# RG-LRU constants made beside S5's first parameters, the first layer norm by ScalarE's square root, and Newton's step on one column with one tensor operand

## The chip, the core and the metric

The kernel runs on one core of a Trainium2 chip. Its engines are TensorE (PE, with the weight loads shown as PEld), VectorE (DVE), ScalarE (ACT), GpSimd (POOL) and SyncE (SP, which here issues all DMAs). Each engine works through its own list of instructions in a fixed order; engines wait for each other by semaphores. The metric is the device time of one execution in microseconds (us), lower is better.

## The reference, cut to what matters

One layer of a trunk: a projection feeds three mixers side by side, their outputs are normalized in groups and projected back, a layer norm follows, then a gated convolutional MLP and a second layer norm. Input and output are 1024 tokens of 1024 values in float32.

```python
proj = x @ w_in[l] + b_in[l]
q, k, v, u, xr, gate = jnp.split(proj, SPLITS, axis=-1)
y_attn = sliding_window_attention(rope(q), rope(k), v, attn_sinks[l])
y_s5  = s5_mixer(u, ...)          # complex diagonal state space model, 16 groups of 64 states
y_lru = rg_lru_mixer(xr, gate, ...)
mix = group_rmsnorm((y_attn, y_s5, y_lru), mix_norm_g[l])
x = layer_norm(ALPHA * x + mix @ w_out[l] + b_out[l], ln1_g[l], ln1_b[l])
f = conv_gated_mlp(x, ...)
x = layer_norm(ALPHA * x + f, ln2_g[l], ln2_b[l])

# in rg_lru_mixer: a constant of each channel, from a_param alone
log_a = -LRU_C * ga * jax.nn.softplus(-a_param)
# in layer_norm
y = xc * lax.rsqrt(var + LN_EPS) * g + b
```

## The kernel before

Matrices are multiplied in three passes over split operands: every float32 operand is a high part `hi`, rounded by ACT, and a low part `lo`, the difference, made mostly by DVE (`split`, L115 to L123: ACT at L119, DVE at L120), and `mm3` (L140) issues hi x hi, lo x hi and hi x lo (L144 to L146). A projection weight is loaded as `wraw`, then split into `whi` and `wlo` (`wsplit`, L166).

The kernel starts with the projection of `u`, the input of S5 (L1292 to L1309), then runs the other projections one half of 512 tokens at a time (`project`, L1319; order in `ORDER`). The work of the mixers is cut into steps of generators, and `AGENDA` says after which projection or attention unit each step is taken (`side`, L1384). `self.after(...)` ties the instructions written inside it to an earlier instruction for the planner only: no semaphore comes of it.

The order on each engine is made by a planner when the kernel is built. It takes ready instructions, those written earlier first, by its own picture of the times, and it hands out tile buffers too. Small tiles (up to 64 bytes in a partition) come from one pool of 64 buffers, by `self.small`.

S5's parameters are made in `s5` (L242), a generator. Its first part (L242 to L263) makes `s5dt`, `s5ang`, `s5n`, `s5r` and `s5x` from the packed parameters, its second (L264 to L274) sines, `decay` and a reciprocal, its third (L275 to L306) the powers `s5Pr`, `s5Pi` and the input matrix `s5Br`, `s5Bi`. The fourth and fifth (L308 to L317) make `s5CA` and `s5W`, 1024 columns each: three operations of each product on DVE (L228 to L230), three on POOL (L231 to L233), and `s5CAi` is negated on DVE at L313. PE then multiplies them at L331 (`s5kp`) and transposes at L341 (`s5wt`).

`lru_setup` (L530) makes the constants of the RG-LRU from two columns: an exponential (`acc_exp`, L200, tiles `lre`), a reciprocal and a polynomial, 33 small DVE instructions and one DMA. They are needed by the gates of `lru` (L582). The call stands at L1313, behind S5's third part (L1312) and the second weight split (L1311).

For a norm, `ln_stats` (L838) makes the mean and variance and a first guess of the reciprocal root, either by POOL's power (`pow`, L797) or by ACT's square root and DVE's reciprocal (L845, L846); `newton` (L800) then improves it by one step. The first layer norm (L1408 to L1417) takes the power, the second (L1496, L1514) the root. In the first, each block of 128 rows goes through `out_group`, statistics, guess, Newton and a normalization (L1416); PE then transposes the block in `x1_block` (L858), and its transposed form feeds the MLP. In the second norm `norm` (L1452) makes `lnm`, lets ACT scale the block, and DVE and POOL take one half of it each (L1462, L1463); the last block is finished by DVE alone (L1515 to L1524).

Of the kernel before, what the change touches and what calls it, by code (L numbers as in the profile page):

```python
# [15 lines left out]
MULT, ADD, SUB, MAX, MIN = ALU.mult, ALU.add, ALU.subtract, ALU.max, ALU.min  # L16
# [41 lines left out]
ALPHA = 2.0 ** 0.25  # L58
LN_EPS = 1e-5
# [18 lines left out]
class Trunk:  # L78
# [721 lines left out]
    def newton(self, r, a):  # L800
        v = self.nc.vector
        t = self.small(list(a.shape), "rst")
        if a.shape[1] == 1:
            v.scalar_tensor_tensor(t, r, a, r, MULT, MULT)
        else:
            v.tensor_tensor(out=t, in0=r, in1=a, op=MULT)
            v.tensor_tensor(out=t, in0=t, in1=r, op=MULT)
        v.tensor_scalar(t, t, -0.5, 1.5, MULT, ADD)  # L808
        v.tensor_tensor(out=r, in0=r, in1=t, op=MULT)

# [417 lines left out]
    def mixers(self):  # L1228
# [7 lines left out]
        r = self.r  # L1236
# [14 lines left out]
        def load_w(h, a, b):  # L1251
            if a == 0:
                ws[h] = self.big([128, NK, 128], "uraw")
            return nc.sync.dma_start(out=ws[h][:, a:b], in_=I["w_in"][6 + h][:, a:b])
# [8 lines left out]
        first = load_w(0, 0, 2)  # L1263
# [15 lines left out]
        def u_out(h, hf, p):  # L1279
            nc.scalar.activation(ud[h][:, :, hf * 64:hf * 64 + 64], p.rearrange("p (c j) -> p j c", j=T5),  # L1280
                                 AF.Identity, bias=self.col("b_in", 6 + h))

        def u_half(h, hf):
            u_out(h, hf, self.proj_half(W[h], self.X, hf, "pud"))
        gs5 = self.s5(ud)
        for f, *a in ((split_w, 0, 0, 2), (split_x, 0, 0), (split_w, 1, 0, 2), (split_w, 0, 2, NK), (split_x, 0, 1),
# [3 lines left out]
            first = self.hi  # L1290
# [11 lines left out]
        self.wsplit(1)  # L1302
        with self.after(first.ins):
            next(gs5)
        u_half(0, 1)
        self.s5_bounce(0, ud[0])
        next(gs5)
# [2 lines left out]
        W = None  # L1310
        self.wsplit(2)  # L1311
        next(gs5)  # L1312
        with self.after(first.ins):  # L1313
            self.lru_setup()
        xr, self.gg, self.q = [], [], []
        steps = [(n[:-1], int(n[-1]), ORDER[:j].count(n)) for j, n in enumerate(ORDER)]
        at, done, Ws = {}, {}, {}
# [66 lines left out]
        def side(t):  # L1384
            with self.after(self.mm.ins):
                for n, g in gens.items():
                    for _ in range(AGENDA[n].count(t)):
                        next(g, None)
# [19 lines left out]
        for tb in range(NB):  # L1408
            self.out_group((0, 1, 2, 3), Wa, MA, r[0], tb)
            z = self.z[tb]  # L1410
            bn = self.small([128, 2, 6], "st")
            for h in range(2):
                nc.vector.bn_stats(bn[:, h], z[:, h * 512:(h + 1) * 512])
            mv, a, rs = self.ln_stats(bn, LN_EPS / ALPHA ** 2)
            self.newton(rs, a)
            nc.vector.tensor_scalar(z, z, mv[:, 0:1], rs, SUB, MULT)  # L1416
            side(100 + tb)  # L1417

    def ffn(self, out):
        nc = self.nc  # L1420
        v = nc.vector
# [24 lines left out]
        st, bn = {}, {}  # L1446
# [5 lines left out]
        def norm(tb):  # L1452
            z = self.z[tb]
            mv, a, r = st[tb]
            self.newton(r, a)
            m = self.small([128, 1], "lnm")
            v.scalar_tensor_tensor(m, mv[:, 0:1], -1.0, r, MULT, MULT)
            o = self.big([128, D], "o")
            for h, e in enumerate((v, nc.gpsimd)):
                s = hs[h]  # L1460
                nc.scalar.activation(z[:, s], z[:, s], AF.Identity, scale=r, bias=m)
                e.tensor_tensor(out=z[:, s], in0=z[:, s], in1=g2[:, s], op=MULT)  # L1462
                e.tensor_tensor(out=o[:, s], in0=z[:, s], in1=b2[:, s], op=ADD)  # L1463
                if tb == 2:
                    nc.sync.dma_start(out=out[0, tb * 128:(tb + 1) * 128, s], in_=o[:, s])
            if tb != 2:
                nc.sync.dma_start(out=out[0, tb * 128:(tb + 1) * 128, :], in_=o)

        cut = nd - self.LAST
        for i in range(cut):  # L1470
# [28 lines left out]
            if p == 3 and 0 < f < 5:  # L1499
                with self.after(self.mm.ins):  # L1500
                    norm(3 + f)
        T = ps["T"]
        self.d_parts(nd)
        for c in range(4):
            last = c == 3
            for k, s in enumerate((slice(0, 256), slice(256, 512)) if last else (hs[0],)):
                for i in range(cut, nd):
                    self.d_product(i, T, (c,), False, i == nd - 1, s)
                    if i == cut and c and not k:
                        with self.after(self.mm.ins):  # L1510
                            norm(c - 1)
                self.d_out(3, c, T, s)
                stats(c, 1 + k, slice(512 + s.start, 512 + s.stop))
            st[c] = self.ln_stats(bn[c][:, 0:2 + last], LN_EPS, True)  # L1514
        tb = 3  # L1515
        z = self.z[tb]
        mv, a, r = st[tb]
# [82 lines left out]
```

## Time and profile before

| | |
|---|---|
| median of 3 runs | 1032.95 us (1032.45 to 1208.34) |
| the profiled execution | 1030.83 us, span of its instructions 1028.9 us |
| PE busy | 969.5 us |
| DVE busy | 770.3 us |
| POOL busy | 557.1 us |
| ACT busy | 488.0 us |

The span runs from the first to the last instruction; the execution's own time has a little around it. Busy time counts what an engine executes, waits for a busy memory interface included, so a DVE instruction can look long because it stood still. A timeline row gives the start and the length in us, the engine, the line of the kernel, the operation, the tile written and the tiles read, shapes, the number of instructions merged in the row, and in brackets the idle time in front of it and what ended it.

### The profile page before, as it was taken

The page shows a single profiled execution, that of the slowest core. Times are in us where ns is not written, and L with a number is a line of the kernel's source. Part 1 is how long each engine was busy: PE and PEld are TensorE (multiplying, and loading weights), DVE is VectorE, ACT ScalarE, POOL GpSimd, SP SyncE. Part 2 cuts the span into 40 slices and gives each one's busy share as a digit, 9 for nine tenths or more (in the row PEclk, how much of TensorE's full clock was granted, in tenths as well). Part 3 has the DMA queues.
Part 4 walks back from the last instruction along what each step waited for, and adds up shares of the span by engine and source line. Part 5 has one row for each costly group of instructions (what it writes and reads, how often), then busy time and mean ns, then how long its engine had stood idle before and what let it go on. Part 6 is the DMA issues. An engine that isn't in the chain of part 4 may idle for free.

```text
span 1028.9 us, 13343 instructions
## 1 busy us (share of the span) xinstructions
PE 969.5 (94%) x4512; PEld 794.4 (77%) x4512; DVE 770.3 (75%) x1254; ACT 488.0 (47%) x943; POOL 557.1 (54%) x417
## 2 busy tenths in 40 slices
PE   9699889989999898899999999999999999999993
PEld 6588757879888676678878778888887788888873
DVE  6969767699888777677677677665676699965298
ACT  6121258667762675535435445445447265444131
POOL 0504405559944684767886978653561799000053
PEclk9899889999999999999999999999999999999997
DMA  8413483443231201447546546412415798686113
GB/s 298 143 42 85 112 205 97 113 129 113 83 124 46 99 20 42 154 161 268 206 162 245 226 154 244 156 59 95 147 78 184 284 391 276 213 293 189 62 42 122
DMA packets 64740, 158.53 MB, mean 154 GB/s; under 512 B 9440, under 2 KB 14080, under 8 KB 64672
## 3 DMA queue, kind: packets, MB, share of 16 engines
q1 hardware_dynamic: 64672, 157.68, 44.8%
q8 instruction: 35, 0.57, 0.2%
q14 instruction: 33, 0.27, 0.1%
HBM read 104.90 MB, written 42.21 MB: 143 GB/s over the span
## 4 chain that ended last, share of the span: by engine, by line
PE 49%; DVE 16%; POOL 13%; DMA 9%; issue 8%; ACT 5%; SPq 1%; DVEq 0%; POOLq 0%; ACTq 0%
PE pg L144 7%; PE pg L146 6%; PE pg L145 6%; PE pdT L145 3%; DMA d<-in_ffn_w_down_dram 3%; PE pdT L146 3%; PE pdT L144 3%; PE pdQ L144 2%; PE pdQ L146 2%; POOL dt L1126 2%; PE pdQ L145 2%; POOL d L1126 2%; PE pin L146 1%; PE pin L144 1%; PE pin L145 1%
## 5 line engine op out<-in xcount | busy, mean ns | idle before, releaser
L120 DVE TENSOR_TENSOR dpl<-draw,dph 128x1024 fp32r<-128x1024 f32 x77 | 120.1, 1598 | 30.1 <-ACT dph L119 28.3
L144 PE MATMUL pg<-xt,apart 128*128 128x512 f32 x352 | 137.3, 391 | 3.6 <-ACT foa L1004 1.4
L145 PE MATMUL pg<-xt,apart 128*128 128x512 f32 x352 | 137.3, 390 | 1.4 <-DVE xt L930 1.4
L146 PE MATMUL pg<-xt,apart 128*128 128x512 f32 x352 | 136.3, 391 | 2.0 <-DVE apart L120 1.9
L119 ACT ACTIVATE dph<-draw 128x1024 fp32r<-128x1024 f32 x77 | 80.1, 1058 | 86.6 <-DVE dpl L120 28.1
L120 DVE TENSOR_TENSOR apart<-s,apart 128x512 fp32r<-128x512 f32 x88 | 93.0, 1067 | 25.3 <-ACT apart L119 25.3
L144 PE MATMUL pg<-xb,apart 128*128 128x512 f32 x264 | 103.2, 391 | 1.4 <-ACT fob L1004 1.4
L145 PE MATMUL pg<-xb,apart 128*128 128x512 f32 x264 | 102.8, 389 | 0.0
L146 PE MATMUL pg<-xb,apart 128*128 128x512 f32 x264 | 102.7, 389 | 0.0
L119 ACT ACTIVATE apart<-s 128x512 fp32r<-128x512 f32 x88 | 53.8, 625 | 84.5 <-POOL s L939 62.4
L144 PEld LDWEIGHTS pg<-xt,apart 128*128 128x128 f32 x352 | 66.1, 188 | 19.7 <-ACT foa L1004 3.6
L146 PEld LDWEIGHTS pg<-xt,apart 128*128 128x128 f32 x352 | 66.1, 188 | 18.3 <-DVE apart L120 4.9
L1462 POOL TENSOR_TENSOR z<-z,ln_g 128x512 f32<-128x512 f32 x7 | 10.9, 1556 | 124.9 <-DVE rst L808 111.4
L145 PEld LDWEIGHTS pg<-xt,apart 128*128 128x128 f32 x352 | 66.1, 188 | 15.8 <-DVE xt L930 2.3
L120 DVE TENSOR_TENSOR apart<-raw,apart 128x512 fp32r<-128x512 f32 x66 | 71.4, 1082 | 5.7 <-ACT apart L119 5.7
L145 PE MATMUL pdT<-dpl,dph 128*128 128x512 f32 (+1 forms) x182 | 69.9, 384 | 2.2 <-DVE dpl L120 2.2
L146 PE MATMUL pdT<-dph,dpl 128*128 128x512 f32 (+1 forms) x182 | 69.4, 382 | 0.0
L144 PE MATMUL pdT<-dph 128*128 128x512 f32 (+1 forms) x182 | 66.7, 383 | 0.7 <-DVE z L1203 0.5
L144 PEld LDWEIGHTS pg<-xb,apart 128*128 128x128 f32 x264 | 49.6, 188 | 12.6 <-ACT fob L1004 2.2
L146 PEld LDWEIGHTS pg<-xb,apart 128*128 128x128 f32 x264 | 49.6, 188 | 10.3
L145 PEld LDWEIGHTS pg<-xb,apart 128*128 128x128 f32 x264 | 49.6, 188 | 10.2
L1060 POOL TENSOR_TENSOR fc<-fc,fob 128x512 f32<-128x512 f32 x11 | 18.7, 1702 | 71.2 <-DVE fob L1003 62.8
(482 smaller groups left out, 2627.0 us busy)
## 6 DMA issues: line engine op xcount, KB each, us to landing
draw<-h SPq DMA_DIRECT2D x77, 256.0 KB, 5.4
raw<-in_ffn_w_gate_dram SPq DMA_DIRECT2D x22, 512.0 KB, 5.0
raw<-in_ffn_w_up_dram SPq DMA_DIRECT2D x22, 512.0 KB, 4.2
h<-fc SPq DMA_DIRECT2D x22, 512.0 KB, 2.6
d<-in_ffn_w_down_dram SPq DMA_DIRECT2D x22, 512.0 KB, 6.6
draw<-d SPq DMA_DIRECT2D x44, 256.0 KB, 5.4
draw<-in_ffn_w_down_dram SPq DMA_DIRECT2D x33, 256.0 KB, 5.4
h<-hs SPq DMA_DIRECT2D x11, 512.0 KB, 3.6
```

Of the source, the lines that this page charges most:

```text
L119: self.hi = nc.scalar.activation(hi, src, AF.Copy)
L120: e.tensor_tensor(out=lo, in0=src, in1=hi.bitcast(F32), op=SUB)
L144: self.mm = nc.tensor.matmul(out, ah, bh, start=first, stop=False, skip_group_check=more)
L145: nc.tensor.matmul(out, ah, bl, start=False, stop=False, skip_group_check=more)
L146: nc.tensor.matmul(out, al, bh, start=False, stop=last, skip_group_check=more)
L1060: e.tensor_tensor(out=c[:, one], in0=c[:, one], in1=x, op=MULT)
L1126: sub = lambda o, a, b: po.tensor_tensor(out=o, in0=a, in1=b, op=SUB)
L1462: e.tensor_tensor(out=z[:, s], in0=z[:, s], in1=g2[:, s], op=MULT)
```

## The change

Four edits. `lru_setup` is called right behind S5's first part, under the same `after`, and no longer behind its third part. The first layer norm passes `True` to `ln_stats`: ACT's square root and DVE's reciprocal take the place of POOL's power. In `newton`, where the operand has one column, the three instructions become `tensor_scalar` with one tensor operand and the others as per-partition scalars; operands of four columns keep theirs. In the second norm `lnm` is made in the same way.

```diff
@@ newton @@
         if a.shape[1] == 1:
-            v.scalar_tensor_tensor(t, r, a, r, MULT, MULT)
-        else:
-            v.tensor_tensor(out=t, in0=r, in1=a, op=MULT)
-            v.tensor_tensor(out=t, in0=t, in1=r, op=MULT)
+            v.tensor_scalar(t, r, a, r, MULT, MULT)
+            v.tensor_scalar(t, t, -0.5, 1.5, MULT, ADD)
+            v.tensor_scalar(r, r, t, None, MULT)
+            return
+        v.tensor_tensor(out=t, in0=r, in1=a, op=MULT)
+        v.tensor_tensor(out=t, in0=t, in1=r, op=MULT)
         v.tensor_scalar(t, t, -0.5, 1.5, MULT, ADD)
         v.tensor_tensor(out=r, in0=r, in1=t, op=MULT)
@@ mixers @@
         self.wsplit(1)
         with self.after(first.ins):
             next(gs5)
+            self.lru_setup()
         u_half(0, 1)
@@
         self.wsplit(2)
         next(gs5)
-        with self.after(first.ins):
-            self.lru_setup()
@@ first layer norm @@
-            mv, a, rs = self.ln_stats(bn, LN_EPS / ALPHA ** 2)
+            mv, a, rs = self.ln_stats(bn, LN_EPS / ALPHA ** 2, True)
             self.newton(rs, a)
@@ norm, second layer norm @@
-            v.scalar_tensor_tensor(m, mv[:, 0:1], -1.0, r, MULT, MULT)
+            v.tensor_scalar(m, mv[:, 0:1], r, -1.0, MULT, MULT)
```

## Rows read from the trace of the kernel before

**Rows 1.** The page, busy us, share of the span, instructions of engines.

```profile
PE 969.5 (94%) x4512; PEld 794.4 (77%) x4512; DVE 770.3 (75%) x1254; ACT 488.0 (47%) x943; POOL 557.1 (54%) x417
```

**Rows 2.** Waits of PE, whole span: us in total, times, longest us.

```profile
PE pin L146 <- DVE wlo L120: 7.9, 1, 7.9
PE xp L109 <- DVE z L1416: 6.2, 3, 3.8
...
PE pdT L145 <- DVE dpl L120: 2.2, 2, 1.7
```

**Rows 3.** Windows: length, busy PE, PEld, DVE, ACT, POOL, PEclk, DMA share, GB/s.

```profile
354.00:359.00 5.00, 4.14 (x16) 3.52 (x17) 2.42 (x8) 2.81 (x8) 0.63 (x2) 0.66 0.44 183
45.00:55.00 10.00, 4.93 (x12) 3.87 (x13) 9.41 (x26) 0.00 (x0) 5.61 (x8) 0.50 0.16 64
```

**Rows 4.** Timeline of PE in the projections, columns as told above.

```profile
50.07 0.79 PE L146 MATMUL pin<-xah,wlo 128*128 128x512 f32 x1 [7.88 <-DVE wlo L120]
...
71.59 0.41 PE L331 MATMUL s5kp<-s5CAi,s5B 128*32 128x128 f32 x2
```

**Rows 5.** Timeline of DVE in the same stretch.

```profile
26.17 0.16 DVE L262 TENSOR_TENSOR s5x<-s5dt,s5lr 128x8 f32<-128x8 f32 x1
...
26.72 0.17 DVE L206 TENSOR_SCALAR s5e_x<-s5x 128x8 f32<-128x8 f32 x1
...
27.95 1.18 DVE L213 SCALAR_TENSOR_TENSOR s5e_p<-s5e_p,s5e_r 128x8 f32<-128x8 f32 x6
...
32.76 0.16 DVE L539 TENSOR_SCALAR lrn<-pack 128x2 f32<-128x2 f32 x1
...
38.27 0.28 DVE L233 TENSOR_TENSOR s5Bi<-s5Bi,s5bbt 128x128 f32<-128x128 f32 x1
...
40.69 7.13 DVE L213 SCALAR_TENSOR_TENSOR lre_p<-lre_p,lre_r 128x2 f32<-128x2 f32 x6
...
48.80 1.21 DVE L120 TENSOR_TENSOR wlo<-wraw,whi 128x1024 fp32r<-128x1024 f32 x1
49.94 0.15 DVE L546 TENSOR_SCALAR lrp<-lrq 128x2 f32<-128x2 f32 x1
50.00 0.15 DVE L550 TENSOR_SCALAR lrs<-lrn 128x2 f32<-128x2 f32 x1
...
65.36 0.69 DVE L313 TENSOR_SCALAR s5CAi<-s5CAi 128x1024 f32<-128x1024 f32 x1
```

**Rows 6.** Timeline of POOL in the same stretch.

```profile
33.16 1.94 POOL L231 TENSOR_TENSOR s5CAi<-s5Pr,s5pack 128x1024 f32<-128x1024 f32 x1 [18.85 <-DMA s5U<-du]
...
45.25 2.33 POOL L233 TENSOR_TENSOR s5Wi<-s5Wi,s5wt 128x1024 f32<-128x1024 f32 x1
```

**Rows 7.** Timelines of DVE and POOL in the first layer norm.

```profile
341.48 0.15 DVE L808 TENSOR_SCALAR rst<-rst 128x1 f32<-128x1 f32 x1
341.67 1.03 DVE L809 TENSOR_TENSOR rs<-rs,rst 128x1 f32<-128x1 f32 x1
...
341.39 1.29 POOL L938 TENSOR_TENSOR s<-raw 128x512 f32<-128x512 f32 x1
```

**Rows 8.** Timeline of DVE at the first norm's sixth block.

```profile
347.51 0.15 DVE L843 TENSOR_SCALAR lna<-mv 128x1 f32<-128x1 f32 x1
...
351.37 0.67 DVE L804 SCALAR_TENSOR_TENSOR rst<-rs,lna 128x1 f32<-128x1 f32 x1 [2.21 <-POOL rs L798]
```

**Rows 9.** ACT: its timeline before the blocks; line L845, ns min/median/max.

```profile
327.07 1.16 ACT L119 ACTIVATE apart<-s 128x512 fp32r<-128x512 f32 x2 [20.59 <-POOL s L941]
...
L845 ACT ACTIVATE rs<-lna x8: 185/202/203, 983.1 to 1020.5; 128x1 f32<-128x1 f32 x8
L845 ACT ACT_TABLE_LOAD  x1: 1283/1283/1283, 956.8 to 956.8; - x1
```

**Rows 10.** Line L804, ns min/median/max; timeline of DVE in the tail.

```profile
L804 DVE SCALAR_TENSOR_TENSOR rst<-rs,lna x16: 203/680/1327, 316.5 to 1022.8; 128x1 f32<-128x1 f32 x16
...
1022.85 1.21 DVE L804 SCALAR_TENSOR_TENSOR rst<-rs,lna 128x1 f32<-128x1 f32 x1
```

## The prediction

> **What bounds the kernel now.** I read the page's busy table first: TensorE (PE) works 94% of the span [rows 1]. So a saving anywhere else is worth only what it takes out of PE's remaining idle time, or off the last microseconds, in which PE has nothing left. Next I read PE's waits [rows 2], longest first, to see which idle time the change can reach. Three entries matter. One wait of 7.9 us is for `wlo`, the low part of a projection weight made by VectorE (DVE). Three waits, 6.2 together and 3.8 the longest, are for `z`, the row block normalized by the first layer norm. Two waits, 2.2 together, are for `dpl` near the end. Then the windows [rows 3]: behind the first wait the granted clock is 0.50 for ten microseconds with 4.93 us of matmuls, behind the 3.8 us wait it is 0.66 over five. PE's two levels are 1.2 and 2.4 GHz; in both stretches it fell after PE had stood still and came back once PE worked again. Work at the lower level takes twice as long, so the first stretch lost 4.93 / 2 = 2.5 us and the second (3.4 of 5 us at half speed) 1.7. What can be won is thus 7.9 + 2.5 = 10.4 at the first place, 6.2 + 1.7 = 7.9 at the second, and something in the tail. All of it would be 1.8% of the time and a little.
>
> **Why wlo is late.** In DVE's timeline [rows 5] the first instruction of `lru_setup` (`lrn`) starts at 32.76, and `wlo` follows only at 48.80, behind most of it. Six instructions of the exponential take 1.18 us for S5 at 27.95 (0.20 each, one waiting for the other), and the same six take 7.13 us for the RG-LRU at 40.69. What differs is POOL: its products and differences over 1024 columns run nearly back to back from 33.16 on [rows 6] (first and last of six). One POOL instruction that runs from 341.39 for 1.29 us shows the rule [rows 7]: a one-column instruction with one tensor operand takes 0.15 us beside it, the next one, with two, takes 1.03 and ends when POOL's ends. So a two-tensor instruction waits for POOL's to end.
>
> **Part 1, lru_setup moved.** Its DMA stays early (weights `lw`, one issue, needed only by the gates much later). Its 33 DVE instructions move ahead of S5's second part, into a stretch in which POOL stands still: no waits there. But they don't come free. In [rows 5] `s5e_x` of S5's second part needs only `s5x` (26.17), yet starts at 26.72; and `lrs` needs only `lrn` (32.76), yet starts at 50.00, right behind `lrp` (49.94). The planner hands out small tiles in the order of the program's first writes. Moved, `lrs` stands ahead of all of S5's second part, so that part starts behind `lrp`, the 20th of a chain in which each instruction waits for the one before: 26.3 + 20 x 0.20 = 30.3, against 26.72. I take S5 as 3.7 us late: its third part ends at 38.55 + 3.7 = 42.2, POOL's products start at 36.9. Bounds: 0 (fully interleaved) and 6.2 (33 x 0.20 = 6.6 from 26.3, none shared).
>
> `wlo` no longer stands behind the chain. Its place in the order was some 16 chained instructions (3.2 us) behind S5's third part; that part is 3.7 later, so `wlo` falls just ahead of its end, before 42, when PE wants it (it had stopped at about 42.2, 7.88 before 50.07 [rows 4]). The 7.9 us wait goes and its clock loss too: PE is 10.4 ahead, and would want S5's `s5CAi` at 71.59 - 10.4 = 61.2 [rows 4].
>
> What is late next is just that tile. From `wlo` at 48.80 to the end of its last step L313, 65.36 + 0.69, DVE took 17.3 us; without the last twelve instructions of `lru_setup` (12 x 0.20) 14.9. But before, POOL had finished by then; now DVE's 1024-column instructions meet POOL's two remaining products and two differences, 2 x 1.94 + 2 x 2.33 = 8.5 us [rows 6], and take turns with them. So `s5CAi` is there at 42.2 + 14.9 + 8.5 = 65.6, and PE waits 4.4 us for it. A wait of that size cost 1.7 us of clock in [rows 3]. Part 1 is worth 10.4 - 4.4 - 1.7 = 4.3. Bounds: 10.4 if the turns cost nothing; and with S5 6.2 late `s5CAi` is there at 68.1, which leaves 3.5, less 1.7 of clock, less 1.2 if `wlo` (1.21 [rows 5]) is put ahead of it: 0.6. Everything behind, up to PE's later wait for the S5 state, hangs on these two engines and shifts with them.
>
> **Part 2, first layer norm.** POOL's power is replaced by ScalarE's (ACT) square root, 0.20 us as in the second norm [rows 9], and a reciprocal, one more one-column DVE instruction (0.15 in [rows 7]). The longest wait shows why it helps: `lna` of that block is ready at 347.66, POOL is busy with other work, and DVE stands idle 2.21 us until 351.37 [rows 8]. By ACT the root comes 0.4 us after `lna` if ACT is free; it also copies and scales transposed blocks there, so I allow 1 us of queue. Newton then loses its two waits for POOL (in [rows 7] 0.9 of one). Of the 3.8 us wait 1.0 is left, of the other two 0.5 together: 4.7 saved, and half of the 1.7 of clock: 5.5. What is queued behind the root on ACT are those copies, 0.2 us later each time: nothing against PE's wait. The added table load is 1.28 us [rows 9] and falls into the 20.59 us for which ACT stands idle up to 327.07; without that cover it would cost 1.28 once. Eight roots in the second norm, with Identity and Copy between them, needed one load, so I count one. The Trainium skill (ScalarE: Activation LUTs, "What ACT_TABLE_LOAD costs") puts a switch at 2.66 us with a drain of 1.38 behind the load; the idle time covers that too, and the sum would be the same by either. Bounds: 0 (ACT's queue as long as POOL's) and 7.9.
>
> **Part 3, Newton's step and the shift.** The count stays three instructions plus one. L804 took 0.20 to 1.33 us for the norms [rows 10]; by [rows 7] it will take 0.15 to 0.2. In the tail three of them lie on the chain that ends last, the last at 1022.85, 1.21 long: 3 x 1.0 = 3.0. Part of it the next two-tensor instruction inherits, as POOL's goes on: I keep 2.2. Before that, four norms lie between DVE and the last `dpl`, which PE waits 1.7 for [rows 2]: I keep 1.3. Sum 3.5; bounds 0.5 (nearly all inherited) and 3.0 + 1.7 = 4.7. With pointers in place of immediates a one-column instruction does not stand in the trace; the nearest rows are 0.15 and 1.03 [rows 7], and I take 0.15, as what it streams is one tensor.
>
> **Sum.** 4.3 + 5.5 + 3.5 = 13.3. The profiled execution took 1030.83 (1028.9 and 1.9 around it); the median of the runs is 1032.95, 2.1 above. Against the profiled one 1017.5, against the median 1032.95 - 13.3 = 1019.7. That is the forecast.
>
> **The rivals.** (a) *The turns with POOL cost nothing*: part 1 gives its 10.4, in all 19.4: 1013.6. For it: DVE's queue is full there, and it may pass two instructions per one of POOL's. Against: 7.13 us for six in [rows 5]. (b) *ACT's queue takes POOL's place*: the root stands behind scaled copies, part 2 gives 0.5: 1024.7. For it: ACT is in order and serves the same blocks; against: 20.59 idle shortly before. (c) *The wait moves on*: a freed Newton only hands POOL's lock to the multiply behind it; part 3 gives 0.5: 1022.7. The Trainium skill (SBUF — State Buffer, "Who interferes with whom") states this as a rule: whoever issues first holds the shared pair for the whole instruction and the other fully blocks. The 1.03 us in [rows 7] agrees. Against (c): Newton's results release ACT, which does not wait for POOL. (d) *The change doesn't do what it says*: a pointer operand waits for POOL like a tensor. Then parts 2 and 3 lose their Newton shares, 1.0 and 3.5: 1024.2. (e) *Slower than before*: the moved instructions are not done when POOL starts, and hold S5's third part at 1.0 us more each, as at 40.69. It decides from the point at which S5 is so late that parts 2 and 3 (9.0) are used up: `s5CAi` at 71.6 + 9.0 = 80.6, 15 us later than I count, fifteen such instructions. With 18 of them it is 3 us slower, 1036. Against it: POOL idles until S5's powers are done, and the chain is done first.
>
> **How the numbers follow.** Forecast 0.47, its own range 1015 to 1024; (a) 0.20, (b) 0.14, (c) 0.10, (d) 0.04, (e) 0.05. A measurement of this kernel tells about 2% from no change, that is 20.7 us: 1012.3. Past it leads only (a) with part 2 or 3 at its upper end (at most 10.4 + 7.9 + 4.7 = 23.0), 0.09. Slower by over 2% would need (e) with 36 such instructions, more than there are, and something besides: 0.02. The range goes from 1011, (a) with half of what is left at the ends, to 1029, which takes in (b) and (d) and leaves out most of (e).
>
> **What would show it.** In the profile after: the 7.9 us wait for `wlo` is gone or under 2 us; the six `lre` steps take 1.2 us before 33; a new PE wait for `s5CAr`, `s5Wr` or `s5CAi` of 3 to 6 us stands near 60 to 65; S5's powers end 3 to 4 us later. The waits for `z` sum to under 2 us, no power of `lna` is left on POOL, and one more table load stands near 315. All one-column instructions of Newton are under 0.25 us. It would be wrong if S5 is not late (then nearer 1013), if ACT's roots stand behind copies, or if the planner reorders the mixers elsewhere.

## The result

The changed kernel takes 1018.01 us (median of 4 runs, 1017.32 to 1019.16) against 1032.7 for the kernel before on the same chip. The ratio is 0.9866, interval 0.9846 to 0.9886: 12 to 16 us shorter, less than 2% and clear of no change. One of the four runs of the kernel before took 1208.34 and stands outside the ratio. In the profiled executions the span went from 1028.9 to 1016.5, by 12.4 us. The forecast was 1019.7. Its sum of 13.3 us came out, but two of its three terms did not; the errors went opposite ways, so that it came out this close is in part luck.

The busy table of the page after, beside [rows 1]: TensorE's share rose from 94% to 95%, VectorE has eight instructions more (the reciprocals), ScalarE nine more (eight roots, one table load), GpSimd eight fewer.

```profile
PE 965.5 (95%) x4512; PEld 792.9 (78%) x4512; DVE 769.8 (76%) x1262; ACT 490.2 (48%) x952; POOL 563.2 (55%) x409
```

TensorE's waits after (us in total, times, longest), to be held against [rows 2]:

```profile
PE s5pY L444 <- DMA s5Hs<-s5H: 4.7, 1, 4.7
PE s5pg L469 <- DMA gluw<-in_s_glu_w_dram: 4.1, 1, 4.1
PE xp L109 <- DVE z L1417: 3.0, 2, 2.1
...
PE pdT L145 <- DVE dpl L120: 1.7, 2, 1.3
PE pin L146 <- DVE wlo L120: 1.6, 2, 1.2
...
PE s5kp L331 <- POOL s5B L324: 1.1, 1, 1.1
```

The wait of 7.9 for `wlo` is gone (1.6 in two pieces), the wait for `z` is 3.0 instead of 6.2, that for `dpl` 1.7 instead of 2.2. The two longest waits are now for transfers, of S5's state and of the gate weights; before they were 4.5 and 3.1, so the second took 1.0 back in this execution (over the kernels profiled here it lies between 0.9 and 4.1).

Where the 12.4 us came from is read from three tiles on TensorE in both traces (the view of one tile: count, ns min/median/max, first and last start). Before:

```profile
L109 PE MATMUL xp<-pack,z x64: 270/273/418, 329.2 to 372.0; 128*128 128x128 f32 x64
...
L144 PE MATMUL pdT<-dph x182: 277/389/499, 799.0 to 1012.7; 128*128 128x512 f32 x170, 128*128 128x256 f32 x12
```

After:

```profile
L331 PE MATMUL s5kp<-s5CAi,s5B x16: 269/272/273, 63.8 to 66.7; 128*32 128x128 f32 x16
...
L109 PE MATMUL xp<-pack,z x64: 270/272/330, 322.3 to 361.8; 128*128 128x128 f32 x64
...
L144 PE MATMUL pdT<-dph x182: 278/389/500, 789.5 to 1002.3; 128*128 128x512 f32 x170, 128*128 128x256 f32 x12
```

The first matmul with `s5CAi` starts 7.8 earlier (71.59 in [rows 4], now 63.8), the first transpose of a normalized block 6.9, the last of them 10.2, the first matmul of the down projection 9.5, its last 10.4, and the span ends 12.4 earlier. So in this pair of profiles the moved constants brought 6.9, the first layer norm about 3 of which 2.6 lasted, the end 2.9.

A second profile of the kernel after, taken with its second timing below, has a span of 1012.5. Against the same kernel before, its first transpose is 8.4 earlier, the last 13.2, the first matmul of the down projection 13.5, the end 16.4: shares of 8.4, 5.1 and 2.9. The first two differ by 1.5 and 2.5 between two executions of one kernel; only that of the end is the same in both.

In the first stage, the timeline of VectorE (start, us, engine, line, operation, output from inputs; in brackets idle time before it and what ended it) shows the moved chain free and the products behind it:

```profile
27.72 1.14 DVE L213 SCALAR_TENSOR_TENSOR lre_p<-lre_p,lre_r 128x2 f32<-128x2 f32 x6
...
30.03 0.16 DVE L206 TENSOR_SCALAR s5e_x<-s5x 128x8 f32<-128x8 f32 x1
...
41.37 1.22 DVE L120 TENSOR_TENSOR wlo<-wraw,whi 128x1024 fp32r<-128x1024 f32 x1
42.51 0.28 DVE L233 TENSOR_TENSOR s5Bi<-s5Bi,s5bbt 128x128 f32<-128x128 f32 x1
42.71 1.22 DVE L120 TENSOR_TENSOR wlo<-wraw,whi 128x1024 fp32r<-128x1024 f32 x1
43.84 1.22 DVE L228 TENSOR_TENSOR s5CAr<-s5Pr,s5pack 128x1024 f32<-128x1024 f32 x1
...
47.25 1.22 DVE L229 TENSOR_TENSOR s5wt<-s5Pi,s5Bi 128x1024 f32<-128x1024 f32 x1
50.37 2.88 DVE L120 TENSOR_TENSOR wlo<-wraw,whi 128x1024 fp32r<-128x1024 f32 x1 [1.90 <-ACT whi L119]
53.17 3.41 DVE L230 TENSOR_TENSOR s5CAr<-s5CAr,s5cat 128x1024 f32<-128x1024 f32 x1
...
62.72 0.94 DVE L313 TENSOR_SCALAR s5CAi<-s5CAi 128x1024 f32<-128x1024 f32 x1
```

GpSimd in the same stretch, same columns:

```profile
36.41 1.94 POOL L231 TENSOR_TENSOR s5CAi<-s5Pr,s5pack 128x1024 f32<-128x1024 f32 x1 [22.29 <-DVE s5Pi L233]
...
42.92 7.34 POOL L231 TENSOR_TENSOR s5Wi<-s5Pr,s5Bi 128x1024 f32<-128x1024 f32 x1 [2.63 <-DMA s5U<-du]
...
52.12 3.38 POOL L233 TENSOR_TENSOR s5CAi<-s5CAi,s5cat 128x1024 f32<-128x1024 f32 x1
```

The six steps of `lre` take 1.14 instead of the 7.13 in [rows 5]. Behind them the engines don't take turns at once: from 42.71 to 48.5 VectorE runs five wide instructions at 1.22 each while one product of GpSimd stands for 7.34 us in place of 1.94. Only after VectorE has been idle, at 50.37, do both slow down together (2.88 and 3.41 against 1.22; 3.38 against the 2.33 in [rows 6]).

### The profile page after: what moved, and what is told of

The parts are those of the page before. It is cut to its first block, busy times and chain, and to the rows that moved or that the text cites. A ratio compares the mean times of both kernels' runs of the same rounds, so it can differ in the third digit from the quotient of the medians.

```text
span 1016.5 us, 13355 instructions
## 1 busy us (share of the span) xinstructions
PE 965.5 (95%) x4512; PEld 792.9 (78%) x4512; DVE 769.8 (76%) x1262; ACT 490.2 (48%) x952; POOL 563.2 (55%) x409
## 4 chain that ended last, share of the span: by engine, by line
PE 55%; DVE 17%; POOL 9%; DMA 8%; issue 6%; ACT 4%; SPq 1%; DVEq 0%; POOLq 0%; ACTq 0%
PE pg L144 7%; PE pg L146 7%; PE pg L145 7%; PE pdT L145 3%; DMA d<-in_ffn_w_down_dram 3%; PE pdT L146 3%; PE pdT L144 3%; PE po L144 2%; PE po L146 2%; PE po L145 2%; PE pdQ L145 2%; PE pdQ L146 2%; POOL dt L1128 2%; PE pdQ L144 2%; POOL d L1128 2%
## 5 line engine op out<-in xcount | busy, mean ns | idle before, releaser
L119 ACT ACTIVATE apart<-s 128x512 fp32r<-128x512 f32 x88 | 53.9, 626 | 63.8 <-POOL s L941 62.4
L144 PEld LDWEIGHTS pg<-xb,apart 128*128 128x128 f32 x264 | 49.6, 188 | 12.6 <-ACT fob L1006 2.2
L1062 POOL TENSOR_TENSOR fc<-fc,fob 128x512 f32<-128x512 f32 x11 | 18.7, 1702 | 71.2 <-DVE fob L1005 62.8
L1086 DVE SCALAR_TENSOR_TENSOR fc<-pg,pack,fc 128x511 f32<-128x511 f32 (+1 forms) x64 | 46.4, 742 | 15.1 <-ACT tail L1083 10.9
L146 PEld LDWEIGHTS pg<-xb,apart 128*128 128x128 f32 x264 | 49.6, 188 | 10.3
```

Of the source, the lines that this page charges most:

```text
L119: self.hi = nc.scalar.activation(hi, src, AF.Copy)
L144: self.mm = nc.tensor.matmul(out, ah, bh, start=first, stop=False, skip_group_check=more)
L146: nc.tensor.matmul(out, al, bh, start=False, stop=last, skip_group_check=more)
L1062: e.tensor_tensor(out=c[:, one], in0=c[:, one], in1=x, op=MULT)
L1086: v.scalar_tensor_tensor(c[:, o + d:o + 512], g[:, 0:512 - d], cw(k), c[:, o + d:o + 512], MULT, ADD)
```

## The experiments

Each kernel was timed beside the kernel before; ratios are to that. Times in us.

**The three parts alone.** First the move alone: kernel before, with `self.lru_setup()` called behind S5's first part.

```
             next(gs5)
+            self.lru_setup()
         u_half(0, 1)
...
-        with self.after(first.ins):
-            self.lru_setup()
```

> The kernel before with lru_setup moved behind S5's first part, and nothing else. Theory A (each edit works at its own place, and the three add up): PE is 7 us ahead from the S5 products on and stays so: 6 to 8 us faster, the 7.9 us wait for wlo gone, the waits for z (6.2) as before. Rival P (the planner's new order elsewhere made the gain): the wait for wlo goes, but the total lies anywhere from 2 slower to 12 faster. Rival T (DVE and POOL take turns, as forecast): 4.3 us faster, with a PE wait of about 4 us at s5kp.

Measured 1023.8, ratio 0.9934 (0.9921 to 0.9947): 6.8 shorter, 5.5 to 8.1. The wait for `wlo` has left TensorE's long waits, that for `z` is untouched; its row in this kernel:

```profile
PE xp L109 <- DVE z L1415: 6.2, 3, 3.8
```

So part 1 by itself gives more than the 4.3 forecast, with less than the 10.4 that lay there.

The root alone: kernel before, with the first layer norm's `ln_stats` taking ScalarE's square root.

```
-            mv, a, rs = self.ln_stats(bn, LN_EPS / ALPHA ** 2)
+            mv, a, rs = self.ln_stats(bn, LN_EPS / ALPHA ** 2, True)
```

> The kernel before with the first layer norm by ACT's square root, and nothing else. Theory A: 1 to 4 us faster; the roots wait 1 to 2 us on ACT behind copies of transposed blocks, Newton's two-operand instructions still wait for POOL, the waits for z fall from 6.2 to 3 or 4. Rival R (the root alone was worth the forecast 5.5): 5 to 6 us faster. Rival N (all of it came from Newton): 0.

Measured 1028.42, ratio 0.9983 (0.9969 to 0.9996): 1.8 shorter, 0.4 to 3.2. Its waits:

```profile
PE xp L109 <- DVE z L1416: 3.9, 3, 2.1
...
PE pg L145 <- DVE xt L930: 1.7, 2, 1.4
```

2.3 of the 6.2 are saved, and 0.3 are given back at the next stage's operand `xt` (1.4 before).

Newton's step alone: kernel before, with the one-column branch of `newton` and the shift `lnm` in pointer form.

```
-            v.scalar_tensor_tensor(t, r, a, r, MULT, MULT)
+            v.tensor_scalar(t, r, a, r, MULT, MULT)
+            v.tensor_scalar(t, t, -0.5, 1.5, MULT, ADD)
+            v.tensor_scalar(r, r, t, None, MULT)
...
-            v.scalar_tensor_tensor(m, mv[:, 0:1], -1.0, r, MULT, MULT)
+            v.tensor_scalar(m, mv[:, 0:1], r, -1.0, MULT, MULT)
```

> The kernel before with Newton's step and lnm on one column with one tensor operand, and nothing else. Theory A: 2.5 to 3.5 us faster, 2 of it behind the last matmul, 0.7 at PE's wait for the last dpl; the 7.9 and 6.2 us waits of PE about as before. Rival N: 5 to 6 us, with the waits for z down to 3. Rival I (the wait moves on to the next two-tensor instruction): under 1 us.

Measured 1026.59, ratio 0.9966 (0.9953 to 0.9978): 3.5 shorter, 2.3 to 4.8. Its waits:

```profile
PE xp L109 <- DVE z L1418: 3.4, 2, 3.0
PE pg L145 <- DVE xt L932: 3.0, 2, 2.7
```

It saves 2.8 of the wait for `z`, but 1.6 of that comes back at `xt`; the wait for `dpl` is 1.5 instead of 2.2. The three alone make 6.8 + 1.8 + 3.5 = 12.1, together 13.8 by the ratio: within the errors they add up, and no gain has to be sought in the reordering that any edit causes elsewhere.

**Is the root worth more beside the other two?** Kernel after, without its root.

```
-            mv, a, rs = self.ln_stats(bn, LN_EPS / ALPHA ** 2, True)
+            mv, a, rs = self.ln_stats(bn, LN_EPS / ALPHA ** 2)
```

> Kernel after, with the first layer norm's root back on GpSimd: the moved constants and the Newton step alone. Theory A (the three parts add up): 1.7 to 3 us slower than the kernel after, 1019.7 to 1021; TensorE's wait for the normalised z is 3.4 (2, 3.0) as with the Newton step alone. Rival F (with the other two parts in place the root is worth the 5.5 us of the forecast): 1023 to 1024. Rival W (the Newton step had already taken what the root could give): within 0.7 us of the kernel after.

Measured 1020.95, ratio 0.9913 (0.9895 to 0.993). Against the 0.9866 of the kernel after that is 4.8 us with an error of 2.7, which leaves both 2.4 and 5.5 open (against the second timing of the kernel after, 0.9879, it is 3.5 with an error of 3.5). Its waits are more exact: 3.4 for `z` and 3.1 for `xt`, sum 6.5, against 3.0 and 1.1, sum 4.1, after. By them the root adds 2.4 to Newton, most of it at `xt`.

**What kept the root's gain short?** First ScalarE's queue was made shorter: kernel after, with the copies `xb` from `xf` on VectorE.

```
-                    nc.scalar.activation(hi, f, AF.Copy)
+                    nc.vector.tensor_copy(out=hi, in_=f)
```

> Kernel after, with the copies xb<-xf (21 of 0.47 us in ScalarE's 325 to 365) made on VectorE, so that ScalarE's queue in the stretch of the first layer norm is shorter by 8 us of 35. Theory Q (the root's gain stayed short because the square roots stand behind copies in ScalarE's queue): from lna to the square root 0.3 to 0.9 us instead of 1.06 to 2.15, TensorE's wait for z 3.0 falls to 2.0 or less, and the time is 0.7 to 2 us shorter, 1016 to 1017.3. Rival V (what is left is VectorE's own chain of reciprocal, Newton, z, each behind other instructions of VectorE): the square roots come sooner but the wait for z stays at 2.5 or more, and the time is within 0.7 us or, with 21 more copies on VectorE, 1 to 2 us longer.

Measured 1025.07, ratio 0.9959 (0.9944 to 0.9973): 8 to 10 us slower than the kernel after by the ratios. The wait for `z` is 9.3 (3, 4.7). The copies are the reason; this is their group on VectorE in the 50 us of that stage (count, busy us, mean ns, idle before):

```profile
L886 DVE CAST xb<-xf 128x256 fp32r<-128x256 f32 x22 | 12.9, 600 | 0.6 <-ACT xf L882 0.5
```

The quickest takes 0.23, the mean is 0.6 and the longest of all 24 takes 1.38; the long ones lie beside GpSimd's instructions. In the last four blocks the root starts 0.18, 0.71, 1.26 and 1.16 us after `lna` does, against 2.15, 1.07, 1.06 and 1.64 in the kernel after, so three of the four come sooner (in the first four it is 0.2 to 0.4 in both); but what is gained there is lost many times over on VectorE, which has no room in this stage. That is the second reason in the expectation, at a higher price than it named, and the queue's own share stays hidden.

Then the root was taken out instead: kernel after, with `r` started from a constant. The normalized values are others then, and the time is read for the wait alone.

```
-            self.nc.scalar.activation(r, a, AF.Sqrt)
+            if eps == LN_EPS:
+                self.nc.scalar.activation(r, a, AF.Sqrt)
+            else:
+                v.tensor_scalar(r, a, 0.0, 1.0, MULT, ADD)
             v.reciprocal(r, r)
```

> Kernel after, with the first layer norm's square root left out: r starts from a constant that VectorE writes in one instruction of the same shape, so the normalised values are other ones and the time is read for the wait alone. Reciprocal and Newton stay. Theory Q (the rest of the wait for z is the root standing in ScalarE's queue): TensorE's wait for z falls from 3.0 to under 1.2 and the time by 1.5 to 3 us below the kernel after. Rival V (the rest is VectorE's own chain of statistics, Newton and z among its other instructions): the wait stays at 2 or more and the time is within 1 us of the kernel after.

Measured 1014.91, ratio 0.9856 (0.9824 to 0.9889). The kernel after, timed in the same set:

> The kernel after, unchanged, timed beside the others of this call. Every theory: 0.986 to 0.989 of the kernel before.

It took 1018.02, ratio 0.9879 (0.985 to 0.9908), so the 3.1 between the two medians lie within the errors. The row of the next stage's operand among the waits without the root:

```profile
PE pg L145 <- DVE xt L935: 2.6, 3, 2.0
```

No wait for `z` is left among the waits, all 3.0 are gone; 1.5 come back at `xt` (1.1 after). So what the change left of the wait for `z` is indeed the way over ScalarE, and VectorE's own chain of reciprocal, Newton and `z` would be in time without it.

**What made wlo late, and the products slow?** Kernel before, with the constants where they were, but with GpSimd's half of S5's products given to VectorE.

```
-..., sh, "s5ca", eng2=po)
+..., sh, "s5ca")
-..., sh, "s5w", eng2=po)
+..., sh, "s5w")
```

> Kernel before, with the halves of S5's products that GpSimd makes given to VectorE, so that GpSimd is still while VectorE makes the RG-LRU constants; their place is that of the kernel before. Theory A (the stretched exponent and TensorE's wait for wlo come from GpSimd's products at the same buffers): the six steps of lre take 1.0 to 1.3 us instead of 7.13, the wait for wlo falls from 7.9 to under 3; VectorE has GpSimd's products to make as well, six of some 1.2 us each, so that S5's matrices come 1 us sooner to 5 us later, and the time is 1025 to 1036. Rival I (the wait comes from the number of instructions ahead of wlo in VectorE's order, not from GpSimd): the steps take 1.2 but wlo is still waited for by 5 us or more at the same place, and the time is 1033 to 1038.

Measured 1022.09, ratio 0.9927 (0.9907 to 0.9946): 7.5 shorter, beyond the expected range at the fast end. VectorE, which now makes twelve wide products instead of six, is done earlier than before:

```profile
35.47 1.25 DVE L213 SCALAR_TENSOR_TENSOR lre_p<-lre_p,lre_r 128x2 f32<-128x2 f32 x6
...
56.48 1.22 DVE L233 TENSOR_TENSOR s5Wi<-s5Wi,s5wt 128x1024 f32<-128x1024 f32 x1
57.61 0.69 DVE L313 TENSOR_SCALAR s5CAi<-s5CAi 128x1024 f32<-128x1024 f32 x1
```

With GpSimd's products gone, the same six steps in the same place of the program take 1.25 instead of 7.13, all products 1.22, the last of them ends at 57.70, not at 62.90, and L313 comes at 57.61, not at 65.36 [rows 5]. TensorE's wait for `wlo` is 2.0. So the cause named in the prediction, GpSimd's wide instructions beside VectorE's, is shown: taking away either the chain or GpSimd removes it, and each is worth about 7 us (6.8 and 7.5).

Both at once, kernel after with the same two arguments taken out:

> Kernel after, with the halves of S5's products that GpSimd makes given to VectorE, as was done to the kernel before in e6_s5_on_dve. Theory C (moving the constants and taking GpSimd out remove one and the same loss, GpSimd and VectorE at the same buffers): the two do not add; the product s5CAr and its five neighbours take 1.22 us each, L313 comes at 56 to 59 instead of 62.7, and the time is 0 to 3.5 us below the kernel after. Rival S (two losses that add): 6 to 7 us below it. Rival D (VectorE is now what the time waits for, since it makes GpSimd's half as well): up to 4 us above it.

Measured 1014.75, ratio 0.9845 (0.9821 to 0.9869), the shortest of all, though its interval overlaps that of the kernel after in the same set. L313 comes at 57.71, as expected, and the products take 1.21 to 1.31. By the ratios the gain over the kernel after is 2.2 or 3.5, by which of its two timings is taken, with errors of 3.2 and 3.9: not clear of none, and the time alone barely excludes 6 to 7. The trace says it more plainly: the products are done at 57.79, as in the kernel before without GpSimd's (57.70), so moving the constants as well brings S5 no sooner. The two edits remove one and the same loss. TensorE's other waits move: 6.5 instead of 4.7 for S5's state to come back through memory, 3.8 instead of 1.7 for `whi` of ScalarE, and 0.9 instead of 4.1 for the gate weights.

**How late is S5?** Kernel after, with the constants' small tiles in buffers of their own, so that they share none with S5's:

```
-        v, S = nc.vector, self.small
+        v = nc.vector
+        S = lambda sh, n, dt=F32: self.cst.tile(sh, dt, name=n)
```

> The changed kernel, with the small tiles of lru_setup each in a buffer of its own, so that S5's second part need not stand behind them in the hand-out. If that order of the hand-out is what made S5 late: POOL's first product starts near 33 and no longer at 36.4, and s5e_x starts near 26.7 and no longer at 30.0. Theory A: PE had only 1.1 us to wait at that place, so at most 1 to 2 us faster. Rival S (S5's 3.3 us are on the path up to PE's wait for s5Hs): 3 to 4 us faster. If the hand-out is not the cause, s5e_x stays at 30.

Measured 1015.73, ratio 0.9856 (0.9842 to 0.9869). S5's second part (`s5e_x`) starts at 27.59 instead of 30.03, GpSimd's first product at 34.01 instead of 36.41, L313 at 60.84 instead of 62.72. So of the 3.3 us by which the move delays S5's second part (26.72 in [rows 5], 30.03 after) 2.4 come from the order in which shared small tiles are handed out; the other 0.9 stay. The medians are 2.3 apart, the ratios 1.0, and the intervals of the two ratios overlap, so that no gain in time is shown. In this kernel VectorE and GpSimd took turns from the start, which they had not done in the kernel after (the next product took 2.95); VectorE's timeline:

```profile
39.16 4.10 DVE L120 TENSOR_TENSOR wlo<-wraw,whi 128x1024 fp32r<-128x1024 f32 x2
```

The same buffers with S5's products on VectorE as well:

> Kernel after, with the RG-LRU constants in buffers of their own as in e4_own and S5's products all on VectorE as in e9_after_dve. Theory C: S5's first product starts 2 to 2.5 us sooner than in e9_after_dve, as e4_own's did against the kernel after; if TensorE still waits for S5's matrices then, the time falls by 1 to 2.5 us below that of e9_after_dve. Rival P (TensorE has other work until then, or waits for S5's states instead): within 0.7 us of e9_after_dve.

Measured 1015.35, ratio 0.9853 (0.9827 to 0.9879). L313 comes at 55.6, 2.1 before that of the kernel with the products alone on VectorE, and the first matmul with `s5CAi` at 62.9 against 63.0: no gain. From there on TensorE has other work until then.

Last, the constants one call earlier, ahead of S5's first part:

```
+            self.lru_setup()
             next(gs5)
-            self.lru_setup()
```

> Kernel after, with the RG-LRU constants made one call earlier, ahead of S5's first part instead of behind it. Theory A (from GpSimd's first product on, each us by which S5's constants come sooner or later moves the end by about as much, since TensorE is short of other work until they are there): the constants' instructions may fill VectorE's idle at 18.6 to 19.6, where it waits for S5's parameters, or go ahead of S5's; GpSimd's first product starts at 34 to 38 (36.4 in the kernel after), and the time moves with it: 1015.5 to 1020. Rival X (the place among S5's first parts is of no matter once the constants are ahead of GpSimd's products): within 0.7 us of the kernel after, whatever the start of the first product.

Measured 1015.07, ratio 0.9866 (0.9846 to 0.9886), the same ratio as the kernel after. GpSimd's first product starts 0.85 sooner (35.56) and `s5CAi` is taken up 0.9 sooner (62.9): the stage follows the first product, as the first theory has it, but so small a step is not told apart from none in the time.

## Why the prediction was right in its sum, and wrong in its terms

**Why wlo is late: right.** Both halves of the reading were tested: GpSimd's wide instructions stretch the chain (7.13 to 1.25 with GpSimd's products gone), and the wait for `wlo` hangs on it.

**Part 1, S5's delay: right.** Forecast: second part at 30.3, third part's end at 42.2, GpSimd's first product at 36.9. Measured: 30.03, 42.8, 36.41. Also as forecast, `wlo` stands just ahead of that end, at 41.37.

**Part 1, what is late next: the step that failed.** The forecast had `s5CAi` ready at 65.6, with 8.5 us of turns between VectorE and GpSimd, a wait of 4.4 for it and 1.7 of clock. Ready it was at 62.72 + 0.94 = 63.66, that is 20.9 behind the third part's end, so the turns cost 6.0 beyond the 14.9 and not 8.5: they were charged from the first product on, and in the trace VectorE ran five wide instructions without one. The larger error is in what TensorE lost by it, 4.4 + 1.7 in the forecast. Its timeline there:

```profile
60.58 0.62 PE L331 MATMUL s5kp<-s5CAr,s5B 128*32 128x128 f32 x4 [1.10 <-POOL s5B L324]
...
63.80 0.38 PE L331 MATMUL s5kp<-s5CAi,s5B 128*32 128x128 f32 x2
```

TensorE waits 1.10, for GpSimd's small copies of `s5B` that stand behind its stretched products, and then is busy up to `s5CAi`. The granted clock stays at its full level, as the windows show (length; busy time of TensorE, its weight loads, VectorE, ScalarE, GpSimd; granted clock; DMA share; GB/s), where it was 0.50 in the ten microseconds of [rows 3]:

```profile
42.00:51.00 9.00, 9.00 (x42) 7.44 (x41) 7.10 (x8) 2.33 (x3) 8.08 (x2) 1.00 0.47 169
51.00:64.00 13.00, 11.90 (x63) 9.46 (x62) 13.00 (x20) 2.66 (x3) 11.89 (x10) 1.00 0.10 21
```

In this execution TensorE was 1.4 late at the start of the projections already (32.12 against 30.69; over the kernels profiled that start lies between 30.2 and 32.2, and the early wait for `xah` between 0.7 and 1.8). Late by 1.4 and held for 1.1, it came to `s5CAi` just as that was ready: the 2.5 by which the tile is behind 61.2, and no more, are what it lost. Of 10.4 that leaves 7.9, where 7.8 were read above; up to the first transpose 0.9 more went, the gate weights among it. The second profile of the kernel after shows that the late start only hid waits: there the projections start at 30.34, and TensorE waits 1.0 for `wlo`, 1.8 for `s5B` and 0.6 for `s5CAi` (ready at 64.46, taken up at 64.61; the view puts this wait down to another tile of VectorE), 3.4 in all, at the full clock again. So the failed terms are the wait of 4.4, of which 2.5 to 3.4 came, in several small pieces, and the clock loss of 1.7, of which nothing came. The sign "a new wait of 3 to 6" missed for this reason. Rival (a), that the turns cost nothing, does not hold either: they cost 6.0, but the small pieces cost no clock.

**Part 2: the term was too large in its waits, by 1.2, and its clock share was not a mechanism.** Forecast 5.5, of it 4.7 in waits and 0.85 in clock. In waits the stage gave 3.2 at `z` and 0.3 at `xt` (3.1 and 0.3 in the second profile); what is left at `z`, 3.0, misses the sign "under 2". The forecast allowed 1 us from `lna` to the root; ScalarE's timeline shows why that was short (the block's `lna` was ready at 332.24):

```profile
332.25 1.60 ACT L882 ACTIVATE xf<-xp,pack 128x128 f32<-128x128 f32 x4
333.61 0.85 ACT L886 ACTIVATE xb<-xf 128x256 fp32r<-128x256 f32 x2
334.23 0.33 ACT L847 ACTIVATE rs<-lna 128x1 f32<-128x1 f32 x1
```

Six of these copies went ahead, and the root started 2.0 us late. On VectorE the last step of Newton then stood behind instructions of the next block until 336.70, so `z` was done at 338.92:

```profile
338.98 1.09 PE L109 MATMUL xp<-pack,z 128*128 128x128 f32 x8 [2.11 <-DVE z L1417]
```

This is one of the two waits that are left, and in this execution clock is lost behind it as behind the long one before: 0.76 in the window.

```profile
338.00:345.00 7.00, 6.02 (x24) 4.95 (x25) 5.04 (x10) 5.29 (x16) 7.00 (x8) 0.76 0.23 93
```

A quarter of 7 us is 1.7, the very sum that the 3.8 us wait had cost. But the second profile of the same kernel has the same wait, and no loss behind it:

```profile
337.53 1.10 PE L109 MATMUL xp<-pack,z 128*128 128x128 f32 x8 [2.13 <-DVE z L1417]
...
336.00:343.00 7.00, 5.47 (x28) 4.68 (x29) 5.64 (x11) 5.84 (x18) 7.00 (x8) 1.00 0.18 75
```

So whether a wait of 2.1 costs clock differs from one execution to the next. The forecast took half of the 1.7 as saved, as if the loss went with the length of the wait; in one profile nothing of it was saved, in the other all, and that is most of why the stage's share is 2.6 in the one and 5.1 in the other. Rival (b) was true in part: ScalarE's queue took GpSimd's place for some of the blocks, and without the root the wait vanishes altogether. The added table load (1.283) did lie in idle time, at 297.5 rather than in the stretch named.

**Part 3: right in its mechanism, and nearly in size.** Forecast 3.5, alone measured 3.5 (2.3 to 4.8); in the kernel after the end gave 2.9, in both profiles. The pointer form never waited; these are all 24 of its first instruction, with the second pointer form below (ns min/median/max):

```profile
L804 DVE TENSOR_SCALAR rst<-rs,lna x16: 255/268/274, 311.9 to 1010.9; 128x1 f32<-128x1 f32 x16
L804 DVE TENSOR_SCALAR rst<-ra,ssq x8: 257/269/277, 284.6 to 305.1; 128x1 f32<-128x1 f32 x8
...
L806 DVE TENSOR_SCALAR rs<-rs,rst x16: 161/214/217, 314.0 to 1011.4; 128x1 f32<-128x1 f32 x16
```

So rival (d) falls. The value taken, 0.15, was too low for two pointers (0.27) and one (0.21), and the sign "under 0.25" fails for the first, at a price of a tenth of a microsecond. The tail is best read from the chain that ended last (start, share in us, engine, tile, line). Before, its last steps:

```profile
1011.90 1.16 DVE rst L804
...
1017.29 1.15 DVE rst L804
...
1022.92 1.15 DVE rst L804
...
1024.47 0.75 DVE o L1523
```

After:

```profile
1001.50 0.18 DVE rst L804
...
1006.12 0.28 DVE rst L804
...
1011.00 0.20 DVE rst L804
...
1011.66 1.01 DVE o L1524
```

Three steps of 1.15 became 0.18 to 0.28, 2.8 less. Given back are 0.26 at the last two-tensor instruction (0.75 to 1.01), 0.06 at the same operation of a block before it and about 0.05 at each pointer form. From the last `pdT` on the chain (1010.21 before, 999.80 after) to the end of the span, 18.7 became 16.7: 2.0, where 2.2 was forecast. At `dpl` 0.5 came instead of 1.3; alone, Newton made up for that in the first layer norm, which the forecast had counted in part 2. Rival (c), that the wait only moves on, holds for a tenth of it: of 2.8 us the instructions behind inherit 0.32.

**Rival (e)** needed GpSimd to meet the moved chain; `lre` was done at 29.05, GpSimd began at 36.41.

What stays open: whether the root is worth 2.4 us beside the other parts, as the waits say, or more, as the timed difference allows; what decides whether VectorE and GpSimd alternate or one of them is held for several instructions; and why the same wait is followed by a lower clock in one execution and not in another.

## What to carry to other kernels

A wide GpSimd instruction on operands in SBUF is paid for by VectorE as well: where both have many of them, try giving all to VectorE (here worth 7.5 by itself, as much as moving the chain), and put chains of tiny dependent instructions where GpSimd is still. A one-column step written as one tensor with per-partition pointers is safe beside GpSimd, at a tenth of a microsecond. Before a small operation goes to another engine's queue, read what that queue issues in the very microseconds in which its input is ready, not its idle time shortly before; and count a clock loss behind a short wait as something that may or may not come: here 1.7 was lost behind 2.1 us of waiting in one execution and nothing in another.

## What the runs showed of the hardware

Two engines were not faster than one: the last of S5's twelve wide products ends at 59.92 and 60.00 in the two profiles of the kernel after, where VectorE and GpSimd share them, and at 57.79 when VectorE makes all; with the constants in buffers of their own it is 57.73 against 55.69.

Who is held is not fixed. One product of GpSimd stood for 7.34 us in place of 1.94 (7.35 in the second profile) while VectorE had one wide instruction after the other; in the kernel with own buffers the same product took 2.80 and VectorE's pair of `wlo` 4.10. The Trainium skill (SBUF — State Buffer, "Who interferes with whom") says that issue order and not the kind of operation decides who blocks. That the kind does not decide agrees with these traces. Issue order alone does not explain the kernel after: GpSimd's product starts at 42.92, and four products of VectorE that start behind it, at 43.84 to 47.25, run at their full pace ahead of it. None of the traces shows when the pair changes hands.

A single tensor operand protects only the one-column forms, so the rule read in the prediction from [rows 7] holds for one column. In the kernel before, a `tensor_scalar` of the chain with two columns and one tensor operand stands beside GpSimd's product of 38.69:

```profile
38.86 1.80 DVE L211 TENSOR_SCALAR lre_p<-lre_r 128x2 f32<-128x2 f32 x1
```

The wide copy of 128x256 took 0.23 to 1.38 in the kernel with the copies on VectorE, and the scaling L313 over 1024 columns, with one tensor operand, 0.68 in the kernel with S5's products on VectorE and 1.76 in the second profile of the kernel after, beside a GpSimd memset of 1.85 for two. The same page of the Trainium skill names copies, casts and `tensor_scalar` among those that can contend in their two-port modes; these rows agree. The one-column forms of Newton's step never took more than 0.277.
